# Output stage of a hybrid attention layer: SyncE and GpSimd in program order, weight splits spread over the tail of the attention

## The chip, the cores and the metric

The kernel runs on one core of a Trainium2 chip. The metric is the device time of one execution in microseconds. The core has five engines with queues of their own: TensorE (PE in the profile; its weight loads are PEld), VectorE (DVE), ScalarE (ACT), GpSimd (POOL) and SyncE (SP), which issues nearly all transfers here. Each engine runs its queue in order; semaphores let one engine wait for another or for a transfer.

## What is computed

One layer over two sequences, a prompt of 1024 rows and a sample of 2048, each row 1024 wide. The first half of the mixed features comes from a windowed attention, the second from a differential attention with an RMS norm over each head. Cut to what matters here:

```
mod = silu(c) @ w_ada + b_ada            # shift, scale, gate of a sequence
u = x * (1 + scale) + shift
qa, ka, va, ga, qb, kb, vb, gb = split(u @ w_in)
oa = window_gqa(qa, ka, va, sink, rel_bias) * silu(ga)              # 512 columns
ob = rms_norm(diff_attention(qb, kb, vb, ...)) * (1 - lambda_init) * silu(gb)   # 512 columns
h = concatenate([oa, ob]) @ w_out                                    # 1024 x 1024
y = layer_norm(ALPHA * x + gate * h, ln_g, ln_b)
```

Of this, the last two lines and the two products in front of them (the norm's factor and silu(gb)) are the output stage.

## The kernel before, in words

The program runs the projections (L186 to L188), the windowed attention, the differential attention and the output stage, in this order, and passes intermediate results through DRAM: oa (gated result of the windowed attention), ot (the differential attention before its norm), frow (the norm's factor of each row, written by 4-byte stores of f at L894), gb (silu of the gate).

The differential attention is cut into 80 units, 64 of the sample and then 16 of the prompt, in software-pipelined slots. `slot(n, ...)` runs the logits of unit n, the softmax of it, and the transposes (L852), values (L870 to L872) and sums (L885, L887) of units up to 3 slots earlier. The slots 80 to 85 are a tail without logits. In them, `slot` is handed a generator, `other`, and calls `next(other)` four times in each; when the slots are over, the rest of the generator is run out. The generator is `outputs()`.

`outputs()` runs the output stage over 24 tiles of 128 rows: first 16 of the sample (s = 1), then 8 of the prompt (s = 0). Tile t needs:
- `load_rest(t)`: five transfers on SP, ot (L999), frow (L1000, one row broadcast to all 128 partitions), gb (L1001), oa (L1002), 256 KB each in SBUF, and x (L1004), 512 KB. They go into 4 rotating buffers `l0`; x goes into 6 views named vt or ptl.
- `join(t)`: POOL multiplies ot by frow (L1012) and by gb (L1013), ACT rounds each half (L1016, half 0 from oa, half 1 from the product) to the high part, and POOL subtracts it (L1017, twice) for the low part. `os_` has three pairs of views for the results (names Q, pth, ptl).
- `output(B, end)`: two halves of 512 columns, each 24 matmuls of 128x512 (L1042 to L1044, high by high, high by low, low by high, 8 row blocks of w_out) in 16 steps, then on DVE the gate (L1047), the residual (L1048) and the norm's statistics (L1051, L1055, L1057). POOL computes the power for 1/sigma (L1058); DVE (L1080), ACT (L1082) and POOL (L1083) apply the norm to both halves, and SP stores the tile (L1084). Tile 23 has an end of its own (L1060 to L1076). PSUM holds the accumulators of two tiles.

In `output` of tile t, `load_rest(t + 3)` is written behind the third step and `join(t + 1)` behind the fifth.

`stage(ks)` loads rows of w_out (L975), `split_weights(k)` splits row block k into a high and a low part (L989 on DVE, L990 on ACT, L991 on POOL and DVE), `load_gate(s)` loads the gate row (L1023) and `load_norm()` the two norm rows (L1028), each broadcast to all partitions.

What sets the order: the program is written for a tile framework that orders the instructions of each engine by a simulated timeline of its own. Inside `tc.manual_schedule(engines=...)` the named engines keep the order in which the program is written. Before, in the last block this names PE alone, so SP, POOL, DVE and ACT follow the framework's order. A transfer waits on SP for the transfer eight places earlier to have landed, because eight semaphores are used in turn.

Of the kernel before, what the change touches and what calls it, by code (L numbers as in the profile page):

```python
# [15 lines left out]
PSUM = bass.MemoryType.PSUM  # L16
DRAM = bass.MemoryType.DRAM

PE = mybir.EngineType.PE
P = 128  # L20
D = 1024
KC = D // P
# [44 lines left out]
def hybrid_layer(ctx, tc, x_prompt, x_sample, c_prompt, c_sample, w_in, w_out, w_ada, b_ada, ln_g, ln_b,  # L67
# [314 lines left out]
    def project_until(cc, n):  # L382
        while done.get(cc, 0) < n:
            if next(steps, steps) is steps:
                break
# [30 lines left out]
    def load_ada(p):  # L416

        hs = []
        for kq in range(4):
            wt = wa_p.tile([P, 2, 2, 256], F32, tag="wa", name="wa")  # L420
            src = w_ada[kq * 256:(kq + 1) * 256, 0:2 * D].rearrange("(k p) (t n) -> p k t n", p=P, t=2)
            for t in range(2):
                ld = nc.sync.dma_start(out=wt[:, :, t, :], in_=src[:, :, t, p * 256:(p + 1) * 256])
            hs.append(wt)
        wada.append(hs + [ld.ins])
# [31 lines left out]
    load_ada(0)  # L457
    with tc.manual_schedule(engines={PE}):
        project_until(0, 6)
# [37 lines left out]

    with tc.manual_schedule(engines={PE}):
        project_until(0, 7)
# [28 lines left out]
    sst.close()  # L528
    with tc.manual_schedule(engines={PE}):
        project_until(0, 13)  # L530


    def windowed(upto):

        order = [(s, i) for s in (0, 1) for i in range(SEQS[s] // P)]
        NB = len(order)
        Bs, live, wait, n0 = {}, [], [], done.get(2, 0)
        total = (upto - n0) * 32
        Bs[0] = load_block(*order[0])
        count = [0, 0]  # L540

        def beside():
            count[0] += 1
            while count[1] * NB * 16 < count[0] * total and done.get(2, 0) < upto:
                next(steps, None)
                count[1] += 1

        for t in range(NB + 2):
            for n in range(2):
                if t < NB and order[t][0] == 1 and order[t][1] >= 7:  # L550
                    project_until(2, 5)
                f = first(Bs[t], n) if t < NB else iter(())
                for h4 in range(4):
                    next(f, None)
                    beside()
                    for g in list(live):
                        if next(g, live) is live:
                            live.remove(g)
                    beside()
                if t < NB:  # L560
                    wait.append(second(Bs[t], n))
                if len(wait) > 1 or t >= NB and wait:
                    live.append(wait.pop(0))
                if n == 0 and t + 1 < NB:
                    Bs[t + 1] = load_block(*order[t + 1])
        for g in live:
            for _ in g:
                pass
        project_until(2, upto)
# [95 lines left out]
    UPTO = 10  # L665
    with tc.manual_schedule(engines={PE}):
        project_until(1, 13)
# [13 lines left out]

    with tc.manual_schedule(engines={PE}):
        windowed(UPTO)
# [213 lines left out]
    def slot(n, extra, other=None):  # L897
        for j in range(4):
            if extra:
                fill(extra)  # L900
            if n < N:
                logits(n, j)
                prefetch(n, j)
            for g, piece in values_at.get(n, ()):
                if piece % 4 == j:
                    values(g, piece)
            if 0 <= n - LAG < N:
                transpose(n - LAG, j)
            if j == 1 and n in sums_at:
                square_sum(sums_at[n])  # L910
            if other is not None:
                next(other, None)
# [4 lines left out]
    ps_lg.open(lst, space=PSUM)  # L917
    with tc.manual_schedule(engines={PE}):
        for n in range(EARLY):
# [35 lines left out]
    def part():  # L955
        return weight(next(turn))
# [15 lines left out]
    def stage(ks):  # L972
        for k in ks:
            raws[k] = early_p.tile([P, D], F32, tag="wo", name="raw") if k < 4 else row_halves()
            nc.sync.dma_start(out=raws[k], in_=w_out[k * P:(k + 1) * P, :])  # L975
# [7 lines left out]
    def split_weights(k):  # L983
        woH[k], woL[k] = wmem[2 * k](), wmem[2 * k + 1]()
        raw = raws.pop(k)
        for n in range(2):
            ns = slice(n * 512, (n + 1) * 512)
            if k >= 4:
                nc.vector.tensor_scalar(out=raw[:, ns], in0=raw[:, ns], scalar1=wsub, scalar2=None, op0=ALU.mult)  # L989
            nc.scalar.copy(woH[k][:, ns], raw[:, ns])  # L990
            (nc.vector if n else nc.gpsimd).tensor_tensor(  # L991
                out=woL[k][:, ns], in0=raw[:, ns], in1=woH[k][:, ns].bitcast(F32), op=ALU.subtract)

    def load_rest(t):

        s, i = order[t]
        cs = slice(i * P, (i + 1) * P)
        d = dat.next().rearrange("p (n i q) -> p n i q", n=4, i=4)
        nc.sync.dma_start(out=d[:, 1], in_=OT[s][:, :, cs].rearrange("k r t -> r k t"))  # L999
        nc.sync.dma_start(out=d[:, 2], in_=frow[s][:, cs].partition_broadcast(P))  # L1000
        nc.sync.dma_start(out=d[:, 3], in_=GB[s][:, :, cs].rearrange("k r t -> r k t"))  # L1001
        nc.sync.dma_start(out=d[:, 0], in_=OA[s][:, :, cs].rearrange("i r t -> r i t"))  # L1002
        xt = xts.next().bitcast(F32)
        nc.sync.dma_start(out=xt, in_=xs[s][cs, :])  # L1004
        Bs[t] = dict(s=s, i=i, d=d, xt=xt)

    def join(t):

        B = Bs[t]
        d = B["d"]  # L1010
        B["oH"], B["oL"] = [v.rearrange("p (k q) -> p k q", k=KC) for v in os_.next()]
        nc.gpsimd.tensor_tensor(out=d[:, 1], in0=d[:, 1], in1=d[:, 2], op=ALU.mult)  # L1012
        nc.gpsimd.tensor_tensor(out=d[:, 1], in0=d[:, 1], in1=d[:, 3], op=ALU.mult)  # L1013
        for half in range(2):
            hs = slice(half * 4, half * 4 + 4)
            nc.scalar.copy(B["oH"][:, hs, :], d[:, half])  # L1016
            nc.gpsimd.tensor_tensor(out=B["oL"][:, hs, :], in0=d[:, half], in1=B["oH"][:, hs, :].bitcast(F32),  # L1017
                                    op=ALU.subtract)


    def load_gate(s):
        keep[s] = part().bitcast(F32)
        nc.sync.dma_start(out=keep[s], in_=grow[s, :].partition_broadcast(P))  # L1023

    def load_norm():
        for name, v in (("g", ln_g), ("b", ln_b)):
            keep[name] = part().bitcast(F32)
            nc.sync.dma_start(out=keep[name], in_=v.partition_broadcast(P))  # L1028
# [60 lines left out]

    def outputs():  # L1090

        load_rest(0)
        stage((4, 5, 6, 7))
        yield
        for k in range(3):
            split_weights(k)
            yield
        load_gate(1)
        load_norm()
        for k in range(3, 7):  # L1100
            split_weights(k)
            yield
        split_weights(7)
        load_rest(1)
        load_rest(2)
        join(0)
        for t in range(NB):
            if t == 8:
                load_gate(0)
            for j, _ in enumerate(output(Bs[t], t == NB - 1)):  # L1110
                if j == 2 and t + 3 < NB:
                    load_rest(t + 3)
                if j == 4 and t + 1 < NB:
                    join(t + 1)
                yield
            del Bs[t]
            yield
# [5 lines left out]
    lst.close()  # L1123
    ps_po = pool(st, "ps_po", 4, PSUM)
    other = outputs()
    with tc.manual_schedule(engines={PE}):
        for n in range(N, max(sums_at) + 1):
            slot(n, 0, other)
        for _ in other:
            pass  # L1130
# [27 lines left out]
```

## Time and profile before

| | us |
|---|---|
| median of 3 runs | 2199.94 |
| lowest, highest | 2194.16, 2206.9 |
| the profiled run | 2195.32 |
| span of the profiled run | 2193.5 |
| PE busy in it | 2081.7 (95%) |
| DVE, ACT, POOL busy | 1300.9, 1034.6, 1153.6 |

The output stage runs from about 1836 us (its first matmul) to the end, with the attention's tail under its first part. Rows of the profile read: start or time, duration in us, engine and line, out<-in by the names of the program. A mark in brackets at a row's end is the idle time of its engine ahead of it, and what ended it. Waits are told as sum in us, times, and longest.

### The profile page before, as it was taken

The page shows a single profiled execution, that of the slowest core. Times are in us where ns is not written, and L with a number is a line of the kernel's source. Part 1 is how long each engine was busy: PE and PEld are TensorE (multiplying, and loading weights), DVE is VectorE, ACT ScalarE, POOL GpSimd, SP SyncE. Part 2 cuts the span into 40 slices and gives each one's busy share as a digit, 9 for nine tenths or more (in the row PEclk, how much of TensorE's full clock was granted, in tenths as well). Part 3 has the DMA queues.
Part 4 walks back from the last instruction along what each step waited for, and adds up shares of the span by engine and source line. Part 5 has one row for each costly group of instructions (what it writes and reads, how often), then busy time and mean ns, then how long its engine had stood idle before and what let it go on. Part 6 is the DMA issues. An engine that isn't in the chain of part 4 may idle for free.

```text
span 2193.5 us, 32703 instructions
## 1 busy us (share of the span) xinstructions
PE 2081.7 (95%) x11597; PEld 1781.9 (81%) x11597; DVE 1300.9 (59%) x2538; ACT 1034.6 (47%) x2022; POOL 1153.6 (53%) x836
## 2 busy tenths in 40 slices
PE   7999999999999999999999999999999987588998
PEld 4777898888988788888978999999999876466777
DVE  6343124212245666767539999999999974244445
ACT  6211113111035677777428777777778973111221
POOL 3223123222233334433338898888989885455573
PEclk9999999999999999999999999999999998799999
DMA  9676536445449667786524231322214646755531
GB/s 279 178 273 181 161 130 178 120 130 135 149 142 241 181 181 196 199 224 160 158 78 132 75 81 37 98 66 81 75 47 132 113 99 173 145 152 162 168 127 58
DMA packets 340204, 312.46 MB, mean 142 GB/s; under 512 B 32087, under 2 KB 296951, under 8 KB 339657
## 3 DMA queue, kind: packets, MB, share of 16 engines
q1 hardware_dynamic: 340040, 310.37, 51.7%
q8 instruction: 92, 1.51, 0.4%
q14 instruction: 72, 0.58, 0.2%
HBM read 212.70 MB, written 97.60 MB: 141 GB/s over the span
## 4 chain that ended last, share of the span: by engine, by line
PE 74%; DMA 11%; POOL 5%; issue 4%; DVE 3%; SPq 2%; ACT 1%; DVEq 0%; POOLq 0%; ACTq 0%
PE lg L814 13%; PE pj L186 11%; PE pj L187 11%; PE pj L188 11%; PE tp L852 6%; PE ac L872 3%; PE ac L871 3%; PE ac L870 3%; PE lgA L607 3%; PE tp L643 2%; DMA l<-ot 2%; PE ac L635 2%; DMA Q<-qb 1%; PE po L1042 1%; PE ac L634 1%
## 5 line engine op out<-in xcount | busy, mean ns | idle before, releaser
L186 PE MATMUL pj<-uH,wH 128*128 128x512 f32 x1040 | 417.0, 401 | 3.8 <-DVE gg L257 3.8
L188 PE MATMUL pj<-uH,wL 128*128 128x512 f32 x1040 | 407.1, 391 | 0.0
L187 PE MATMUL pj<-uL,wH 128*128 128x512 f32 x1040 | 406.7, 391 | 0.0
L217 POOL TENSOR_TENSOR wL<-wr,wH 128x1024 fp32r<-128x1024 f32 x74 | 181.9, 2459 | 410.0 <-DVE wH L215 367.9
L814 PE MATMUL lg<-kt,Q 128*128 128x512 f32 x1280 | 377.9, 417 | 8.0 <-DMA Q<-qb 5.3
L838 POOL TENSOR_TENSOR l<-l,l 128x1024 f32<-128x1024 f32 x160 | 383.1, 2420 | 0.2
L827 ACT ACTIVATE l<-l,nm 128x2048 f32<-128x2048 f32 (+1 forms) x192 | 331.0, 1724 | 20.0 <-DVE nm L819 19.8
L814 PEld LDWEIGHTS lg<-kt,Q 128*128 128x128 f32 x1280 | 218.1, 190 | 40.4 <-issue 3.9
L819 DVE CUSTOM_DVE_ANT_0 l<-lg,W 128x1024 f32<-128x1024 f32 x192 | 233.4, 1216 | 17.8 <-PE lg L814 17.6
L854 ACT CAST pth<-tp 128x512 fp32r<-128x512 f32 x320 | 186.2, 582 | 115.8 <-PE tp L852 111.9
L836 POOL TENSOR_SCALAR l<-l,s 128x1024 f32<-128x1024 f32 x160 | 179.1, 1134 | 113.2 <-DVE s L832 56.0
L188 PEld LDWEIGHTS pj<-uH,wL 128*128 128x128 f32 x1040 | 195.1, 188 | 42.2
L186 PEld LDWEIGHTS pj<-uH,wH 128*128 128x128 f32 x1040 | 195.5, 188 | 35.8 <-DVE gg L257 4.6
L187 PEld LDWEIGHTS pj<-uL,wH 128*128 128x128 f32 x1040 | 195.8, 188 | 29.6
L855 DVE TENSOR_TENSOR ptl<-tp,pth 128x512 fp32r<-128x512 f32 x320 | 208.9, 684 | 11.3 <-ACT pth L854 10.3
L852 PE MATMUL tp<-ident,l 128*128 128x128 f32 x1280 | 194.9, 276 | 8.7 <-DVE ptl L855 8.6
L870 PE MATMUL ac<-pth,vt 128*128 128x256 f32 x640 | 182.1, 285 | 5.9 <-ACT ac L887 5.9
L622 POOL TENSOR_SCALAR l<-l,rcA 128x384 f32<-128x384 f32 (+1 forms) x144 | 81.1, 581 | 196.5 <-PE ac L634 93.9
L872 PE MATMUL ac<-pth,vt 128*128 128x256 f32 x640 | 183.0, 286 | 0.0
L871 PE MATMUL ac<-ptl,vt 128*128 128x256 f32 x640 | 182.6, 285 | 0.0
L819 DVE CUSTOM_DVE_ANT_0 l<-lg,W,nm 128x1024 f32<-128x1024 f32 x128 | 164.1, 1282 | 23.3 <-PE lg L814 15.9
L852 PEld LDWEIGHTS tp<-ident,l 128*128 128x128 f32 x1280 | 149.9, 142 | 11.8 <-DVE ptl L855 3.8
(209 smaller groups left out, 4048.1 us busy)
## 6 DMA issues: line engine op xcount, KB each, us to landing
wr<-in_w_in SPq DMA_DIRECT2D x39, 1024.0 KB, 5.5
KAt<-ka SPq DMA_DIRECT2D x40, 384.0 KB, 10.0
QAt<-qa SPq DMA_DIRECT2D x24, 512.0 KB, 4.3
kt<-kb SPq DMA_DIRECT2D x24, 512.0 KB, 9.0
Q<-qb SPq DMA_DIRECT2D x48, 256.0 KB, 3.0
Q<-qb SPq DMA_DIRECT2D x96, 128.0 KB, 4.0
vt<-vb SPq DMA_DIRECT2D x48, 256.0 KB, 5.7
out<-vt SPq DMA_DIRECT2D x20, 512.0 KB, 2.6
```

The lines of the kernel that those rows point to most:

```text
L186: nc.tensor.matmul(acc, lhsT=a(k), rhs=b(k), start=(k == 0), stop=False)
L187: nc.tensor.matmul(acc, lhsT=a(k), rhs=bl(k), start=False, stop=False)
L188: nc.tensor.matmul(acc, lhsT=al(k), rhs=b(k), start=False, stop=(k == KC - 1))
L814: nc.tensor.matmul(L[:, c * CH:(c + 1) * CH], lhsT=G["Q"][:, v, m, b * P:(b + 1) * P], rhs=Kt[kt0 + c][:, m, :], start=(v == 0), stop=(v = ...
L819: nc.vector.tensor_tensor_reduce(out=half, in0=L, in1=W[:, off:off + 1024], scale=1.0, scalar=nm[:, m, 0:1] if s and hf else 3e38, op0=ALU ...
L827: nc.scalar.activation(e, e, AF.Exp, bias=nm[:, m, hf:hf + 1], scale=-1.0, accum_out=sums)
L838: nc.gpsimd.tensor_tensor(out=row[:, cs], in0=row[:, cs], in1=rows[n][1][:, cs], op=ALU.add)
L852: nc.tensor.transpose(pt[:, c * P:(c + 1) * P], rows[n][0][:, (j * 4 + c) * P:(j * 4 + c + 1) * P], ident)
L855: nc.vector.tensor_tensor(out=L[:, :, qs], in0=p3, in1=H[:, :, qs].bitcast(F32), op=ALU.subtract)
L870: nc.tensor.matmul(a, lhsT=Vt[kq][:, 0, c, :], rhs=H[:, c, :], start=(kb == 0), stop=False)
L871: nc.tensor.matmul(a, lhsT=Vt[kq][:, 0, c, :], rhs=L[:, c, :], start=False, stop=False)
L872: nc.tensor.matmul(a, lhsT=Vt[kq][:, 1, c, :], rhs=H[:, c, :], start=False, stop=(kb == T - 1))
```

## The change

In `outputs()`, the loads of the rows of w_out 4 to 7 are put before the first `load_rest`. The splits 0 to 3 take a step each, then come the gate row, two empty steps, the norm rows, and another step. The splits 4 to 7 follow at one step each, with join(0) and load_rest(1) behind split 5, and load_rest(2) behind the last. Tile 0 starts after 12 steps instead of 8, in slot 83 instead of 82. And in the last block SP and POOL keep the program's order, like PE; DVE and ACT do not.

```diff
@@ -16,7 +16,7 @@
 PSUM = bass.MemoryType.PSUM
 DRAM = bass.MemoryType.DRAM
 
-PE = mybir.EngineType.PE
+PE, SP, POOL = mybir.EngineType.PE, mybir.EngineType.SP, mybir.EngineType.Pool
 P = 128
 D = 1024
 KC = D // P
@@ -1089,21 +1089,24 @@
 
     def outputs():
 
+        stage((4, 5, 6, 7))
         load_rest(0)
-        stage((4, 5, 6, 7))
         yield
-        for k in range(3):
+        for k in range(4):
             split_weights(k)
             yield
         load_gate(1)
+        yield
+        yield
         load_norm()
-        for k in range(3, 7):
+        yield
+        for k in range(4, KC):
             split_weights(k)
+            if k == 5:
+                join(0)
+                load_rest(1)
             yield
-        split_weights(7)
-        load_rest(1)
         load_rest(2)
-        join(0)
         for t in range(NB):
             if t == 8:
                 load_gate(0)
@@ -1123,7 +1126,7 @@
     lst.close()
     ps_po = pool(st, "ps_po", 4, PSUM)
     other = outputs()
-    with tc.manual_schedule(engines={PE}):
+    with tc.manual_schedule(engines={PE, SP, POOL}):
         for n in range(N, max(sums_at) + 1):
             slot(n, 0, other)
         for _ in other:
```

On SP, at the first store of an output tile: the rows around `out_1`, the sample's output. The names at the left are what is written; l0 with a number is the buffer of one tile's loads, ot1, frow1, gb1 and oa1 are the sample's DRAM tensors, vt and ptl hold x, and ot0 and frow0 belong to the prompt's attention. Before:

```order
L1002 DMA l0_19129<-oa1_99 128x4x128
L999 DMA l0_19064<-ot1_98 128x4x128
L894 DMA frow0_102<-f_19277 128x2x1
L1001 DMA l0_18843<-gb1_97 128x4x128
L999 DMA l0_19129<-ot1_98 128x4x128
L1000 DMA l0_19057<-frow1_103 128x4x128
L1001 DMA l0_19057<-gb1_97 128x4x128
L1084 DMA out_1<-vt_18848 128x1024
L1002 DMA l0_18843<-oa1_99 128x4x128
L1000 DMA l0_19064<-frow1_103 128x4x128
L1004 DMA vt_18848<-in_x_sample 128x1024
L999 DMA l0_18843<-ot1_98 128x4x128
```

After:

```order
L1000 DMA l0_19175<-frow1_103 128x4x128
L1001 DMA l0_19175<-gb1_97 128x4x128
L1002 DMA l0_19175<-oa1_99 128x4x128
L1004 DMA vt_19180<-in_x_sample 128x1024
L876 DMA ot0_81<-osb_19188 128x256
L894 DMA frow0_102<-f_19223 128x2x1
L876 DMA ot0_81<-osb_19247 128x256
L894 DMA frow0_102<-f_19265 128x2x1
L1084 DMA out_1<-vt_18854 128x1024
L999 DMA l0_18849<-ot1_98 128x4x128
L1000 DMA l0_18849<-frow1_103 128x4x128
L1001 DMA l0_18849<-gb1_97 128x4x128
```

Before, the first store stands among loads of four different buffers, in mixed order; now the five loads of a tile stand together, behind the store of a tile before it.

On ACT, from the norm of tile 3 on (`L1016 CAST` is a half of a join, `L1082 ACTIVATE` a half of the norm; l0 with a number is again a buffer of loads). Before:

```order
L1082 ACTIVATE vt_19134<-po_19472,ve_19541 128x512
L1082 ACTIVATE vt_19134<-po_19511,ve_19541 128x512
L1016 CAST ptl_19165<-l0_19129 128x512 x2
L1082 ACTIVATE vt_19322<-po_19552,ve_19621 128x512
L1082 ACTIVATE vt_19322<-po_19591,ve_19621 128x512
L1016 CAST ptl_19330<-l0_18843 128x512 x2
L1082 ACTIVATE ptl_19405<-po_19632,ve_19701 128x512
L1082 ACTIVATE ptl_19405<-po_19671,ve_19701 128x512
```

After:

```order
L1082 ACTIVATE vt_19180<-po_19472,ve_19541 128x512
L1082 ACTIVATE vt_19180<-po_19511,ve_19541 128x512
L1016 CAST ptl_19330<-l0_19075 128x512
L1016 CAST ptl_19204<-l0_19175 128x512
L1082 ACTIVATE vt_19322<-po_19552,ve_19621 128x512
L1082 ACTIVATE vt_19322<-po_19591,ve_19621 128x512
L1016 CAST Q_19067<-l0_19134 128x512
L1016 CAST ptl_19330<-l0_18849 128x512
```

vt_19134 and vt_19180 are tile 3, vt_19322 is tile 4 in both. Before, the two L1016 of one join stand between the norms of two tiles; now there are halves of two different joins: between tiles 3 and 4 half 1 of tile 5 (l0_19075) and half 0 of tile 7 (l0_19175).

On POOL, around the powers of the tiles 3 and 4 (ve_19541 and ve_19621; L1058 is the power, L1083 the norm's last step, L1012, L1013 and L1017 the join). Before:

```order
L1058 TENSOR_TENSOR ve_19461<-ve_19461,mhalf_109 128x1
L1012 TENSOR_TENSOR l0_19057<-l0_19057 128x512
L1083 TENSOR_TENSOR vt_19069<-vt_19069,pth_18949 128x512 x2
L1013 TENSOR_TENSOR l0_19057<-l0_19057 128x512
L1017 TENSOR_TENSOR Q_19072<-l0_19064,Q_19071 128x512 x2
L1058 TENSOR_TENSOR ve_19541<-ve_19541,mhalf_109 128x1
L1083 TENSOR_TENSOR vt_19134<-vt_19134,pth_18949 128x512 x2
L1012 TENSOR_TENSOR l0_19064<-l0_19064 128x512
L1017 TENSOR_TENSOR pth_19166<-l0_19129,ptl_19165 128x512
L1013 TENSOR_TENSOR l0_19064<-l0_19064 128x512
```

After:

```order
L1013 TENSOR_TENSOR l0_18849<-l0_18849 128x512
L1017 TENSOR_TENSOR pth_19205<-l0_18849,ptl_19204 128x512 x2
L1058 TENSOR_TENSOR ve_19541<-ve_19541,mhalf_109 128x1
L1083 TENSOR_TENSOR vt_19180<-vt_19180,pth_19009 128x512 x2
L1012 TENSOR_TENSOR l0_19075<-l0_19075 128x512
L1013 TENSOR_TENSOR l0_19075<-l0_19075 128x512
L1017 TENSOR_TENSOR pth_19331<-l0_19075,ptl_19330 128x512 x2
L1058 TENSOR_TENSOR ve_19621<-ve_19621,mhalf_109 128x1
L1083 TENSOR_TENSOR vt_19322<-vt_19322,pth_19009 128x512 x2
L1012 TENSOR_TENSOR l0_19134<-l0_19134 128x512
L1013 TENSOR_TENSOR l0_19134<-l0_19134 128x512
```

The join of one tile, from L1012 to the second L1017, now stands whole behind the norm of another; before, its parts stand ahead of, between and behind the norm's.

## Rows read from the trace of the kernel before

**Rows 1.** Windows: us, busy time of each engine (instructions), PEclk, DMA share, GB/s

```profile
1836.00:1867.00 31.00, 26.68 (x153) 23.41 (x152) 7.81 (x16) 9.68 (x30) 14.37 (x14) 0.94 0.72 186
1867.00:1906.00 39.00, 19.04 (x82) 14.79 (x80) 15.55 (x28) 3.00 (x6) 14.72 (x14) 0.79 0.76 133
1906.00:2000.00 94.00, 72.59 (x272) 56.91 (x273) 30.78 (x53) 13.75 (x24) 52.59 (x46) 0.87 0.56 155
2000.00:2130.00 130.00, 120.65 (x499) 95.00 (x498) 59.91 (x102) 24.09 (x42) 82.92 (x74) 0.97 0.49 153
```

**Rows 2.** Waits of PE, ACT and POOL in the output stage: total us, times, longest

```profile
PE po L1042 <- ACT vt L1082: 47.1, 11, 23.8
ACT vt L1082 <- POOL ve L1058: 191.5, 16, 32.9
POOL l L1012 <- DMA l<-ot: 110.6, 20, 17.5
```

**Rows 3.** Timeline of SP, and the chain of waits: start us, us, what

```profile
1953.36 0.36 SPq L1000 DMA_DIRECT2D l<-frow  x1
...
1957.06 9.13 DMA l<-ot
```

**Rows 4.** Timeline: the longest wait of POOL, and stores issued on SP

```profile
1893.14 1.26 POOL L1012 TENSOR_TENSOR l<-l 128x512 f32<-128x512 f32 x1 [17.55 <-DMA l<-ot]
1905.73 1.24 SPq L1084 DMA_DIRECT2D out<-vt  x1
2075.79 0.35 SPq L1084 DMA_DIRECT2D out<-vt  x1
2159.08 0.33 SPq L1084 DMA_DIRECT2D out<-vt  x1
2181.28 0.33 SPq L1084 DMA_DIRECT2D out<-vt  x1
2189.77 1.08 SPq L1076 DMA_DIRECT2D out<-ptl  x2
```

**Rows 5.** Transfers issued (1923, 2034, 1982 us on; page): KB, us to landing

```profile
l<-frow SPq DMA_DIRECT2D x1, 256.0 KB, 8.2
l<-frow SPq DMA_DIRECT2D x1, 256.0 KB, 4.7
l<-gb SPq DMA_DIRECT2D x8, 256.0 KB, 3.4
out<-vt SPq DMA_DIRECT2D x20, 512.0 KB, 2.6
```

**Rows 6.** Windows of a few us, columns as above

```profile
1954.00:1960.00 6.00, 2.82 (x9) 1.99 (x9) 3.78 (x7) 2.29 (x4) 5.20 (x6) 0.85 0.24 38
1961.00:1965.00 4.00, 4.00 (x18) 3.21 (x17) 0.00 (x0) 0.00 (x0) 0.00 (x0) 0.93 1.03 339
1996.00:1999.00 3.00, 3.00 (x15) 2.42 (x14) 0.47 (x1) 0.00 (x0) 3.00 (x3) 1.00 0.31 78
```

**Rows 7.** Timeline: single instructions of a tile on POOL, SP and ACT

```profile
2008.33 2.54 POOL L1083 TENSOR_TENSOR vt<-vt,pth 128x512 f32<-128x512 f32 x2
2014.88 0.39 SPq L999 DMA_DIRECT2D l<-ot  x1
2015.15 1.27 ACT L1082 ACTIVATE vt<-po,ve 128x512 f32<-128x512 f32 x2 [10.57 <-POOL ve L1058]
2016.30 1.14 ACT L1016 CAST Q<-l 128x512 fp32r<-128x512 f32 x2
```

**Rows 8.** The attention's tail: a wait of SP, timeline, chain, first output matmul

```profile
SPq L999 <- PE tp L852: 10.1, 1, 10.1
1818.64 1.26 POOL L1012 TENSOR_TENSOR l<-l 128x512 f32<-128x512 f32 x1 [7.80 <-DMA l<-frow]
1836.00 0.48 PE L1042 MATMUL po<-kt,Q 128*128 128x512 f32 x1
1859.21 8.29 DMA frow<-f
1867.99 18.76 DMA frow<-f
```

## The prediction

> **What bounds the kernel now.** I read the windows of the output stage first [rows 1], then the waits of the engines there [rows 2], then the chain [rows 3], and last the rows of single instructions. The windows show that PE is the bound nowhere before 2000 us: from 1867 to 1906 it works 19.04 of 39 us, from 1906 to 2000 72.59 of 94, and from 2000 to 2130 120.65 of 130, where the granted clock is 0.97, so the 2.4 GHz level nearly throughout. The waits say what it lacks. PE waits 47.1 us for free PSUM tiles, which the ACT normalisation at L1082 gives back; ACT waits 191.5 us there for the POOL power at L1058; POOL waits 110.6 us in L1012 for a load [rows 2]. POOL runs in order, and L1012, the first product of a later tile's join, stands ahead of the small power of a tile that is ready, so a late load holds up both. The worst case is the hole of 17.55 us before the L1012 at 1893.14. The first store, out(0), leaves at 1905.73, out(12) at 2075.79, out(20) at 2159.08, and the program's last at 2189.77 [rows 4]. That is 170.1 us for the twelve cycles up to out(12), 14.2 each, 83.3 us for the next eight, 10.4 each, and the rest.
>
> Late loads are the kernel's real price here. The broadcast frow (512-byte pieces, one row for all partitions) is slow: 256 KB of the sample's land 8.2 us after issue, of the prompt's 4.7, whereas 256 KB of gb take 3.4 and a 512 KB store 2.6 [rows 5]. While only a sample's frow is under way (1954 to 1960) the queues move 38 GB/s, with a prompt's (1996 to 1999) 78, and right behind it (1961 to 1965) 339 [rows 6]. Loads of one queue land in the order of issue: the ot issued at 1957.06 landed 9.13 later, at 1966.19 [rows 3]. Behind the frow that left at 1953.36 there were 1.28 MB (oa, x, gb, ot), 3.8 us at 339 GB/s, so this frow landed near 1962.4, 9.0 us after issue. I take 9.0 for the sample's, with 8.2 as the lower bound and 9.7 as the upper (9.13 and half a handover), and 4.7 for the prompt's. What hides this now is that the loads run two or three tiles ahead of their use, in whatever order the scheduler gave SP.
>
> **The change part by part.** *Manual order on SP.* The added load order is strictly out(t-1), then the five loads of tile t+3: ot, frow, gb, oa, x. No load is ahead of a store any more, although nothing but the scheduler's order made it so; the work saved is nil (the same DMAs, 0.35 to 0.4 us of issue each). *Manual order on POOL.* Per tile: L1058, L1083 twice, then the next join's L1012, L1013 and L1017 twice. The long L1012 waits of POOL [rows 2] therefore no longer stand between a finished tile and its power. Alone that would give back up to 110.6 us of POOL wait, of which PE feels only its 47.1 us. *ACT stays with the scheduler, and there a wait appears.* In its new row L1016 of tile t+3, half 0, which reads oa(t+3), stands ahead of the L1082 of tile t. In the old one L1082 stood ahead of it. Now oa(t+3) is issued behind out(t-1), so a loop closes: out(t-1) is issued, oa(t+3) lands, L1016, L1082 and L1083 of tile t run, out(t) is issued. Queued behind the waiting L1016 on ACT are both L1082 of tile t; behind these wait POOL's L1083 and SP's store, and PE for PSUM.
>
> The period of that loop for a sample's tile: two issues up to frow's own 0.9, at some 0.4 each [rows 7], frow 9.0, gb and oa 0.5 MB at 339 GB/s 1.6, one half of L1016 0.6 and one of L1082 0.65, both halves of L1083 2.54 [rows 7], and five handovers of 0.1, which is 15.8 us. (A frow of 8.2 gives 15.0, one of 9.7 gives 16.5.) For a prompt's it is 11.5. PE needs 11.1 per tile ((2181.28 - 2159.08)/2, out(20) to out(22), PE without pause [rows 4]), so the loop is later than PE in both, by 4.7 and 0.4 us.
>
> Stores issued: tiles out(0) to out(12) trigger the loads of tiles 4 to 15, all sample; those up to out(20) the prompt's. Twelve cycles at 15.8 are 190 against 170.1 now: **+19.5**. Eight at 11.5 are 92 against 83.3: **+8.7**. Behind out(20) nothing is loaded any more, and PE, the join and the two last tiles run as they do now: **0**.
>
> *Order in the tail.* Loads of tiles 0 to 3, the gate, the norm rows and the splits are spread; output(0) gets its first PE steps four steps (one slot) later than now. Two stalls go: SP no longer waits 10.1 us at L999 for the transposes of PE at L852, and POOL no longer 7.8 us before L1012 at 1818.64 with L836 behind it. Two come: the loads of the last rows of w_out stand behind stores of f, 4-byte packets, one of which took 8.29 us [rows 8]. I set these against each other at 0, with 6 us either way. Then ACT's L1082 of tile 0 waits, by the same inversion, for oa of tile 3. By then the queue has to move, from about 1841 (when the sums of the slot let SP go on; first output matmul at 1836.00 [rows 8]), gate and norm rows 1.5 MB, tiles 1 and 2 3.0, ot to oa of tile 3 1.0, attention stores 0.4: 5.9 MB. The windows from 1836 to 1906 give (31 x 186 + 39 x 133)/70 = 156 GB/s [rows 1], so 38 us: oa(3) at 1879, out(0) near 1884 instead of 1905.73: **-21.7**. What covers this is that nothing else needs the queue; without the cover (oa(3) only by 1900) the gain is gone.
>
> The sum: -21.7 + 19.5 + 8.7 + 0 = +6.5 us against the profiled run's own 2195.32, of which 2193.5 are span. The three runs' median is 4.6 us above that, so on its scale 2199.94 + 6.5 = **2206**. PE idle of before, 47 us, is not won, because the wait only changes its owner.
>
> The Trainium skill bears on that step ("DMA: Bandwidth & Descriptors", section "Queues, rings and completion order"): descriptors of one ring are consumed in order on each engine. That speaks against the change, since oa must then wait behind out and frow, and rows 3 agree.
>
> **The rivals.** *A, faster: the loop is later than nothing.* If a frow that is alone behind a store lands as other loads of its size do, in 3.4 us, the period is 10.2, below PE's 11.1, and PE sets the pace. Then out(0) at 1884, 20 x 11.1, and 34.4 from out(20) to the end: a span of 2140, a run of 2142, 2147 on the median. For it: frow's neighbours share the 16 engines, and GB/s is high right behind it. Against it: 38 GB/s in a stretch with nothing else in the queue [rows 6]. The Trainium skill has a rule for it, the fit of 2.0 us and bytes/436e3 in "DMA: Bandwidth & Descriptors", "Anatomy of one DMA — SWDGE (gpsimd) path": by it 256 KB take an estimated 2.6 us, and the case would be A. Rows 5 disagree, for gb by 0.8 us and for frow by more. Chance 0.18.
> *M, in between:* frow at the 6 to 7 us of a mean of both kinds, or the loop slackened by a store that leaves early: 13 to 14 us a cycle, and -21.7 - 14 + 8.7 or -21.7 - 2 + 8.7: 2173 to 2185. Chance 0.14.
> *B, slower: out(0) isn't earlier.* SP in the order of the program puts the loads of tiles 1 to 3 behind stores of f, whose data come from DVE and POOL at the end of each slot. Each such store holds SP until its data are there, and the chain has one that took 18.76 us, at 1867.99 [rows 8]. It decides if oa(3) lands after 1900: then the -21.7 falls away, the loop still costs +28, and the time is 2228; with frow at 9.7 2236. Chance 0.18.
> That the change does nothing is excluded, since the rows of SP, POOL and ACT are in another order.
>
> **How the numbers follow.** Forecast 0.50 (2192 to 2220: out(0) 10 us either way, a frow between the bounds), A 0.18, M 0.14, B 0.18. Half a per cent, about what a measurement tells from no change, is 11 us, so same is 2189 to 2211. Faster gets A, nearly all of M, and none of the forecast: 0.31. Of the forecast 0.32 lies within the 11 us and 0.18 above, B lies above: same 0.32, slower 0.37. As both signs have much chance, the range goes from A's 2147 to B's 2232, and 2192 to 2220 is the likeliest case's own.
>
> **What would show it.** Right: ACT's largest wait is L1016 on a load of oa, some 8 us, in twelve tiles; stores out(t) 16 us apart for tiles 1 to 12 and 11.5 after; out(0) near 1884; no POOL wait in L1012 for a load; a granted clock below 0.9 up to out(12), since PE pauses 4.7 us in each tile. Wrong if stores are 11.1 apart from the start (A) or if out(0) leaves after 1895 (B), or if frow in the new queue lands in less than 6 us.

## The result, and the profile after

The changed kernel takes 2262.78 us (median of 4 runs, 2257.25 to 2264.41) against 2197.88 for the one before; the ratio is 1.0285, with a 95% interval of 1.0248 to 1.0322. The forecast was 2206 and the range ended at 2232: the direction was right, the size far too small. The profiled runs differ by nearly as much: spans of 2255.5 and 2193.5 us, 62.0 apart.

First the timeline of SP, the stores of tiles 0, 12 and 20, which answer to the stores of [rows 4].

```profile
1904.25 0.34 SPq L1084 DMA_DIRECT2D out<-vt  x1
...
2110.22 0.35 SPq L1084 DMA_DIRECT2D out<-vt  x1
...
2220.92 0.35 SPq L1084 DMA_DIRECT2D out<-vt  x1
```

They place the loss: the first store comes 1.5 us earlier than before, the twelve cycles up to out(12) take 206.0 us instead of 170.1 (17.2 each), the next eight 110.7 instead of 83.3 (13.8 each), and the rest 34.6 instead of 34.4. -1.5 + 35.9 + 27.4 + 0.2 = 62.0. All of the loss is in the cycles.

The windows of the three stretches, with the columns of [rows 1] (busy us of PE, PEld, DVE, ACT, POOL; PEclk, DMA share, GB/s):

```profile
1836.00:1904.00 68.00, 41.92 (x203) 35.25 (x201) 17.66 (x33) 12.78 (x38) 23.47 (x22) 0.80 0.68 101
1904.00:2110.00 206.00, 154.38 (x576) 119.91 (x576) 70.05 (x120) 28.87 (x48) 95.88 (x85) 0.89 0.48 125
2110.00:2221.00 111.00, 92.95 (x380) 73.08 (x381) 46.63 (x80) 19.25 (x32) 64.69 (x58) 0.97 0.53 152
```

No engine is full, PE pauses about 4.3 us in each of the twelve cycles, and the queues move less than before (125 GB/s against 155 in the third of rows 1). Something is waited for in turn. The waits from out(0) on, ACT's up to out(20), say what; they answer to [rows 2]:

```profile
PE po L1044 <- POOL pth L1017: 49.9, 14, 5.6
PE po L1044 <- POOL Q L1017: 22.1, 7, 5.6
...
POOL vt L1083 <- ACT vt L1082: 131.8, 19, 9.9
POOL ptl L1083 <- ACT ptl L1082: 24.3, 3, 9.5
...
ACT ptl L1016 <- DMA l<-oa: 121.8, 14, 11.0
...
ACT Q L1016 <- DMA l<-oa: 53.9, 6, 10.3
```

POOL's waits in L1012, 110.6 us before, are gone from here on (one of 18.1 us, for a frow, is left in the tail), and PE waits only 0.7 us for PSUM. In their place ACT stands in L1016 for oa 20 times, 175.7 us in all, POOL's L1083 waits for ACT's L1082 behind it, and PE for the join that POOL reaches only then. The chain of waits shows one turn of the loop, from the issue of an oa (2.5 us behind out(3)) to the issue of the next:

```profile
1957.55 11.57 DMA l<-oa
...
1969.23 0.06 ACT ptl L1016
...
1969.75 0.69 ACT vt L1082
...
1971.75 1.27 POOL vt L1083
1973.02 0.02 issue
1973.03 0.35 SPq L1084
...
1974.21 0.60 SPq L1000
1974.81 0.05 issue
1974.86 0.69 SPq L1001
1975.55 0.04 issue
1975.59 11.10 DMA l<-oa
```

The load of oa, one half of L1016, the norm, the store, three issues of loads (ot, frow, gb), and the next load of oa: this is the loop of the prediction, link by link. What is longer than forecast is its first link. The transfers between 1921 and 2112 us (sample) and between 2113 and 2195 us (prompt), with median us from issue to landing, answer to [rows 5]:

```profile
l<-ot SPq DMA_DIRECT2D x12, 256.0 KB, 3.6
l<-frow SPq DMA_DIRECT2D x12, 256.0 KB, 10.6
...
l<-oa SPq DMA_DIRECT2D x11, 256.0 KB, 10.7
...
l<-oa SPq DMA_DIRECT2D x6, 256.0 KB, 7.3
...
l<-frow SPq DMA_DIRECT2D x6, 256.0 KB, 7.1
```

A sample's ot is there 3.6 us after its issue, its frow, issued 0.5 us later, after 10.6: 7.5 us from the one landing to the next.

### The profile page after: what moved, and what is told of

It is laid out like the page before. It is cut to its first block, busy times and chain, and to the rows that moved or that the text cites. A ratio compares the mean times of both kernels' runs of the same rounds, so it can differ in the third digit from the quotient of the medians.

```text
span 2255.5 us, 32659 instructions
## 1 busy us (share of the span) xinstructions
PE 2099.9 (93%) x11597; PEld 1793.1 (80%) x11597; DVE 1296.5 (57%) x2538; ACT 1037.2 (46%) x2022; POOL 1154.6 (51%) x836
## 4 chain that ended last, share of the span: by engine, by line
PE 70%; DMA 16%; SPq 4%; DVE 3%; POOL 3%; issue 2%; ACT 1%; ACTq 0%; DVEq 0%; POOLq 0%
PE lg L814 12%; PE pj L186 11%; PE pj L187 11%; PE pj L188 11%; DMA l<-oa 8%; PE tp L852 5%; PE ac L872 3%; PE ac L871 3%; PE ac L870 3%; PE lgA L607 3%; PE tp L643 2%; DMA Q<-qb 2%; PE ac L635 2%; POOL vt L1083 1%; PE ac L634 1%
## 5 line engine op out<-in xcount | busy, mean ns | idle before, releaser
L814 PE MATMUL lg<-kt,Q 128*128 128x512 f32 x1280 | 377.2, 416 | 8.3 <-DMA Q<-qb 6.1
L814 PEld LDWEIGHTS lg<-kt,Q 128*128 128x128 f32 x1280 | 217.3, 190 | 40.8 <-issue 6.6
L855 DVE TENSOR_TENSOR ptl<-tp,pth 128x512 fp32r<-128x512 f32 x320 | 208.7, 684 | 12.1 <-ACT pth L854 10.8
L852 PE MATMUL tp<-ident,l 128*128 128x128 f32 x1280 | 195.9, 276 | 17.1 <-DVE ptl L855 17.0
```

Source lines behind the costliest of these rows:

```text
L814: nc.tensor.matmul(L[:, c * CH:(c + 1) * CH], lhsT=G["Q"][:, v, m, b * P:(b + 1) * P], rhs=Kt[kt0 + c][:, m, :], start=(v == 0), stop=(v = ...
L852: nc.tensor.transpose(pt[:, c * P:(c + 1) * P], rows[n][0][:, (j * 4 + c) * P:(j * 4 + c + 1) * P], ident)
L855: nc.vector.tensor_tensor(out=L[:, :, qs], in0=p3, in1=H[:, :, qs].bitcast(F32), op=ALU.subtract)
```

## The experiments

Each edit is against the changed kernel unless another is named, and times are medians beside the kernel before on the same chip (2198.56 to 2202.54).

**Which engine's order makes the loss?** Three kernels change only what follows the program.

```diff
-    with tc.manual_schedule(engines={PE, SP, POOL}):
+    with tc.manual_schedule(engines={PE, SP}):        # e_sp
+    with tc.manual_schedule(engines={PE, POOL}):      # e_pool
+    with tc.manual_schedule(engines={PE}):            # e_spread
```

> The changed kernel, but in the last block only PE and SP keep the program's order; POOL goes back to the scheduler. Loop theory (store of tile t-1, then load of tile t+3 on SP, whose oa half ACT rounds ahead of the norm of tile t): the loop needs SP's order and ACT's order, not POOL's, so the stores stay 17 us apart for the sample and 13.8 for the prompt, and the time within 12 us of the changed kernel's 2263. Rival (POOL's order makes the loss): stores 14 us apart as before, near 2200.

Measured: 2272.01 (ratio 1.0319, 1.0298 to 1.034), stores 18.0 us apart up to out(12) and 14.7 behind it. The loss is there without POOL's order. Why each cycle is 0.8 to 0.9 us longer than in the changed kernel was not followed up.

> The changed kernel, but only PE and POOL keep the program's order; SP goes back to the scheduler, which puts the loads of six tiles ahead of the first store and load of tile t+6 behind the store of t. Loop theory: no loop although ACT still rounds half 0 of tile t+3 ahead of the norm of tile t; no ACT wait for oa above 2 us in the steady part, stores at the pace of the transfers, near 13 us for the sample, and at PE's 11.1 for the prompt: 2180 to 2200. Rival (POOL's order makes the loss): stays near 2263.

Measured: 2144.31 (0.9753, 0.9728 to 0.9778), 118 us below the changed kernel and, level with e_poolpad below, the fastest of all. Its window from out(0) to out(20) has PE without a gap:

```profile
1887.00:2108.00 221.00, 221.00 (x956) 179.08 (x955) 116.59 (x199) 50.51 (x80) 161.78 (x139) 1.00 0.68 183
```

From out(1) to out(20) the stores are 10.7 us apart on the mean. This was below the 2180 that I expected: the transfers, which I had put at 13 us a tile, don't set the pace there, they carry 183 GB/s. ACT's order has the same inversion in this kernel; what differs is that the load of tile t+6, not t+3, stands behind the store of t.

> The changed kernel with only PE in the order of the program: the spread of the splits and loads alone. Loop theory: the loads are hoisted again, the stores 14 us apart as in the kernel before, and the time within 20 us of its 2198. Rival (the spread of the splits makes the loss by a late start): first store after 1925 us and a time above 2230.

Measured: 2197.26 (0.9973, 0.9953 to 0.9992): the spread alone does next to nothing, and POOL waits in L1012 for ot again.

```profile
POOL l L1012 <- DMA l<-ot: 106.2, 19, 21.6
```

**Is the loop closed by ACT's order?** Here ACT too follows the program, in which tile t's norm comes behind the join of tile t+1, not behind half of that of t+3.

```diff
-    with tc.manual_schedule(engines={PE, SP, POOL}):
+    with tc.manual_schedule(engines={PE, SP, POOL, ACT}):
```

> The changed kernel, with ACT too in the order of the program, so that ACT rounds tile t+1, not t+3, ahead of the norm of tile t; the orders of SP and POOL stay as changed. Loop theory: the oa in question was issued two stores earlier, the loop is gone, stores near 13 us apart for the sample and 11.1 for the prompt, 2180 to 2200, PE waits for the join under 1 us a tile. Rival (the strict order of SP alone costs it, each load late behind a store whoever waits): ACT or POOL waits for the load instead, stores still 16 us or more apart, over 2240.

Measured: 2163.36 (0.9825, 0.981 to 0.9839), with stores 9 to 12.6 us apart from tile 2 on. In the cycles SP's strict order costs nothing by itself: out(0) to out(20) takes 218.7 us, against 221.3 in e_pool. As with e_pool the pace came out faster than I had expected, and PE sets it (busy for 192.93 of the 193 us from out(2) to out(20)). The time is still 19 us above e_pool's. In the two profiles this lies ahead of out(0), which leaves at 1908.48 here and at 1886.80 there; why was not followed up.

**Can the loop be opened elsewhere?** One kernel loads a tile earlier, one loads oa first.

```diff
-                if j == 2 and t + 3 < NB:
-                    load_rest(t + 3)
+                if j == 2 and t + 4 < NB:
+                    load_rest(t + 4)
...
         load_rest(2)
+        load_rest(3)
```

> The changed kernel with the loads of tile t+4, not t+3, written behind the third step of tile t (and those of tile 3 put with tile 2's). SP, POOL in program order and ACT's inversion stay. Loop theory: the loop now spans two stores, so its period of 17 us is shared by two tiles and PE's 11.1 us decide: stores 11 us apart from tile 2 on, 2155 to 2175 in all. Rival (the order of SP as such costs it): stores stay over 15 us apart, over 2230.

Measured: 2170.2 (0.9866, 0.9847 to 0.9885), stores 11.1 apart from tile 4 on.

```diff
+        nc.sync.dma_start(out=d[:, 0], in_=OA[s][:, :, cs].rearrange("i r t -> r i t"))
         nc.sync.dma_start(out=d[:, 1], in_=OT[s][:, :, cs].rearrange("k r t -> r k t"))
         nc.sync.dma_start(out=d[:, 2], in_=frow[s][:, cs].partition_broadcast(P))
         nc.sync.dma_start(out=d[:, 3], in_=GB[s][:, :, cs].rearrange("k r t -> r k t"))
-        nc.sync.dma_start(out=d[:, 0], in_=OA[s][:, :, cs].rearrange("i r t -> r i t"))
```

> The changed kernel with oa as the first of a tile's five loads instead of the fourth. Every order between tiles stays. Loop theory with the frow as its long term: the loop loses ot, frow and gb, some 8 us of its 17, falls below PE's 11.1, and the time to 2155 to 2180. Rival (the wait is for the store ahead, or a fixed time of any transfer): stores still over 14 us apart, over 2215.

Measured: 2172.42 (0.9871, 0.9855 to 0.9888), stores 11.1 apart from tile 4 on. Moving one line of five takes back all of the loss and more. Both were as expected.

**What in the load is long?** The first kernel replaces the broadcast of frow by a plain load of as many bytes, the second keeps it and sets frow's rows 512 bytes further apart in DRAM.

```diff
-        nc.sync.dma_start(out=d[:, 2], in_=frow[s][:, cs].partition_broadcast(P))
+        nc.sync.dma_start(out=d[:, 2], in_=GB[s][:, :, cs].rearrange("k r t -> r k t"))
```

> The changed kernel with the frow load replaced by a second load of gb's rows, of the same 256 KB without the broadcast (so the norm's factor is left out and the result differs). Theory: the broadcast is the slow part, about 7.5 us between the landings of ot and frow; a load of the plain kind takes 0.9 there, so the period falls from 17.2 to about 10.6 for the sample and below PE's 11.1 for the prompt: stores 11 us apart, 2155 to 2175. Rival (any 256 KB load behind a store takes this long): stores 16 us apart, over 2240.

Measured: 2161.41 (0.9823, 0.9802 to 0.9844), stores 11 to 12 us apart in most cycles. The transfer itself is not slow by its size or its place behind a store.

```diff
-    frow = [dt_([HB, S], f"frow{s}") for s, S in enumerate(SEQS)]
+    frow = [dt_([HB, S + P], f"frow{s}") for s, S in enumerate(SEQS)]
```

> The changed kernel with frow's rows 512 bytes further apart in DRAM (pitch 8704 and 4608 bytes instead of 8192 and 4096). If the pitch makes the sample's broadcast slower than the prompt's, the sample's stores come 14 us apart or less instead of 17.2, and the time falls to 2225 or below. Rival (slow because 128 partitions read the same lines, whatever the pitch): 17 us, within 10 us of 2263.

Measured: 2175.24 (0.9887, 0.9859 to 0.9915), stores 12.3 us apart for the sample and for the prompt. I had given 14. The transfers of this kernel from 1904 to 2088 us:

```profile
l<-ot SPq DMA_DIRECT2D x15, 256.0 KB, 3.6
l<-frow SPq DMA_DIRECT2D x15, 256.0 KB, 5.2
```

The same broadcast of the same bytes lands 5.2 us after issue instead of 10.6, some 2 us behind ot instead of 7.5. So it is the layout of frow in DRAM, with 8192 bytes between the four rows, that makes the sample's broadcast slow. For the prompt's, with 4096 bytes, this trace has no time to landing, but its cycles fell too, from 13.8 to 12.3 us. Only one wider pitch was tried, and why the pitch matters is not shown. The loop is still the bound, since 12.3 is above PE's pace, but at 28% less for the sample and 11% less for the prompt. The Trainium skill has a fact of this kind ("DMA: Bandwidth & Descriptors", section "Latency and other measured facts", row on the pitch of rows at large powers of two): there, copies at pitches of 2 MiB and more are slowed, and 4 KiB added to a pitch of 4 MiB restores their rate, while 192 bytes do not. This case's runs agree in kind (10.6 us to landing against 5.2), at a pitch of 8 KiB and with 512 bytes added, neither of which that row covers.

The kernel before, and then e_pool, with the wider pitch (the same edit):

> The kernel before with the wider pitch alone. If the slow broadcast set its pace of 14.2 us up to out(12) and its late first store, POOL's waits for loads in L1012 fall from 110.6 us to under 50 and the time to 2150 to 2175. Rival (the scheduler's order of POOL sets it): 2185 to 2200.

Measured: 2169.72 (0.9868, 0.985 to 0.9886), inside the range. Up to out(12) the stores came 11.9 us apart instead of 14.2. Out(0) left at 1908.20, but in this run the attention ended late (its last matmuls of logits, L814, start at 1822.44, in the profile of before at 1803.12); from there it is 85.8 us instead of 102.6. POOL's waits for ot fell from 110.6 us only to 62.7, not below 50, so its order keeps a share:

```profile
POOL l L1012 <- DMA l<-ot: 62.7, 18, 5.1
POOL l L1012 <- DMA l<-frow: 23.7, 4, 13.0
```

> PE and POOL alone in the order of the program (2144), with the wider pitch. The stores there are already 10.9 us apart, which is PE's pace, so only the start can gain: out(0) 0 to 15 us before 1886.8, 2130 to 2145.

Measured: 2144.58 (0.9762, 0.9737 to 0.9786), the same as e_pool, at the upper end of what was expected. Out(0) leaves at 1882.78 instead of 1886.80 and the profiled span is 2139.7 instead of 2142.6 us, a gain too small for these runs to tell.

**Does the order in the tail matter?** The old order is put back, once with SP, POOL and PE in the order of the program (e_oldorder), once with POOL and PE (e_oldpool).

```diff
+        load_rest(0)
         stage((4, 5, 6, 7))
-        load_rest(0)
         yield
-        for k in range(4):
+        for k in range(3):
...
-            if k == 5:
-                join(0)
-                load_rest(1)
             yield
+        split_weights(7)
+        load_rest(1)
         load_rest(2)
+        join(0)
```

> The old order of splits and loads in the tail with SP, POOL and PE in the order of the program. Loop theory: the same loop, stores 17.1 and 13.8 us apart, and the time within 25 us of the changed kernel's 2263, by what the tail gives or takes. Rival (the spread is what costs): near 2200.

Measured: 2253.29 (1.0241, 1.022 to 1.0261): stores 17.3 us apart up to out(12) and 13.9 behind it. The loop is the same with the old tail, and the time 9 us lower.

> The old order of splits and loads with PE and POOL in the order of the program, SP with the scheduler. If POOL's order is the gain (the power no longer behind a join that waits for its load), stores 11 us apart and 2140 to 2165; if the spread of the splits is needed for it, above 2180.

Measured: 2149.12 (0.9764, 0.9736 to 0.9791), as with the new tail. POOL has no wait for a load in L1012 in this trace. The gain comes with POOL's order; the spread is not needed for it. With POOL's order set, the scheduler orders SP and ACT otherwise too: SP issues 6 loads of oa ahead of the first store and ACT runs 6 casts (L1016) ahead of the first norm (L1082), where the kernel before has 8 and 8. What this is worth by itself was not separated.

**Why was the first store late?** The tail's stores of f go to ACT's queue (with `tail` set ahead of the last block).

```diff
-        nc.sync.dma_start(out=frow[s][h, i * P:i * P + QG].rearrange("(b p) -> p b", p=P), in_=f[:, 4:6])
+        (nc.scalar if tail else nc.sync).dma_start(out=frow[s][h, i * P:i * P + QG]..., in_=f[:, 4:6])
```

> The changed kernel with the stores of f in the tail's slots issued from ACT's queue instead of SP's. Theory for the start that was not won (the loads of tiles 1 to 3 land in order behind the stores of f on SP's queue, each of which takes 8 to 19 us to land): oa of tile 3 lands some 15 us earlier, so out(0) leaves near 1888 instead of 1904.3, and the loop is as it was: 2240 to 2255. Rival (the queue is slow with the sheer bytes of the tail, 156 GB/s): out(0) within 5 us of 1904, 2257 to 2268.

Measured: 2250.23 (1.0228, 1.0199 to 1.0256), out(0) at 1894.91. I had given 1888. In this run the tail began later than in the changed kernel's, so the start is better counted from a mark. From the same store of f (1820.53 and 1815.13) it is 74.4 us instead of 89.1, 14.7 less, and the wider pitch alone (e_frowpad) gives 71.4. But SP reaches that store only after a wait for POOL, which took 8.4 us here, 6.1 in the changed kernel and 10.8 in e_frowpad. The attention's last matmuls of logits lie ahead of that wait: they start at 1809.41, 1806.33 and 1806.46, and out(0) leaves 85.5, 97.9 and 85.0 us later. So the gain is 12.4 us here and 12.9 with the pitch. SP's waits for the data of f, 17.4 us in three waits up to out(0) of the changed kernel, leave its queue with the stores, so this run does not tell them from the slow landings.

With the wider pitch as well:

> The changed kernel with the wider pitch of frow and the tail's stores of f on ACT's queue. If both held the loads of tiles 1 to 3, out(0) leaves another 5 to 10 us earlier than with the pitch alone (counted from the store of f in slot 80, 71 us there): 60 to 66 us; stores 12.2 apart as with the pitch alone; 2165 to 2172. If the f stores are hidden once the broadcast is quick, 71 us and 2172 to 2178.

Measured: 2178.4 (0.9908, 0.9875 to 0.994), out(0) at 1900.62, 75.4 us behind that store and 86.3 behind the last logits (1814.31). Together they win no more than each alone, as in the second case of the expectation. ACT's timeline at the norm of tile 0 shows why. In the changed kernel:

```profile
1900.42 0.62 ACT L1016 CAST Q<-l 128x512 fp32r<-128x512 f32 x1 [14.03 <-DMA l<-oa]
1900.94 1.26 ACT L1082 ACTIVATE vt<-po,ve 128x512 f32<-128x512 f32 x2
```

And in e_fq, then in e_padfq, where the norm's line is L1084:

```profile
1891.56 1.29 ACT L1084 ACTIVATE vt<-po,ve 128x512 f32<-128x512 f32 x2 [5.26 <-DVE po L1082]
...
1897.28 1.29 ACT L1084 ACTIVATE vt<-po,ve 128x512 f32<-128x512 f32 x2 [5.26 <-DVE po L1082]
```

With the stores of f out of the way, the norm of tile 0 no longer waits for oa of tile 3 but for VectorE's step of the same norm, so an earlier oa of tile 3 has nothing more to give.

And the same edit in e_pool:

> PE and POOL alone in the order of the program (2144), and the tail's stores of f on ACT's queue. If the stores of f hold the loads in the tail, out(0) leaves 5 to 15 us before the 1886.8 of that kernel and the time is 2130 to 2140; if ACT's queue or its own order gets in the way, or the loads weren't late, 2142 to 2155.

Measured: 2163.55 (0.9833, 0.98 to 0.9865), out(0) at 1911.95, a miss: 19 us slower than e_pool. From the last logits to out(0) it is 95.0 us, against 78.5 in e_pool. The store of f on ACT's queue is no gain where SP issues the loads that early. Whether ACT's issue of it or the scheduler's new order did it was not separated.

## Why the prediction was wrong, point by point

**The loop: right, but for one reading.** It was named with its links, its waiting engine and who is held behind it; e_act, e_ahead4 and e_oafirst each open or shorten one link, and the loss is gone each time, while e_sp and e_oldorder keep the links and the loss. ACT's waits for oa came to 8.8 us on the mean, where some 8 were given. The wrong reading is that in ACT's old row the norm of tile t stood ahead of the cast of tile t+3. In the trace of before ACT runs 8 casts, those of four tiles, ahead of the first norm, so the inversion was there already; the changed kernel runs 6 and e_pool 6. What the change added is the place of the load: SP issues 8 loads of oa ahead of the first store before, 4 in the changed kernel, 5 in e_ahead4 and 6 in e_pool. The loop needs both, the cast ahead of the norm and its load right behind the store of the tile before.

**Its period: the step that failed.** The prediction counted 9.0 us for a sample's frow and 4.7 for a prompt's from the frow's own issue. It took them from transfers before [rows 3, 5] that SP had issued 5 us or more behind the transfer ahead of them. In the loop every frow is issued 0.9 us behind a 512 KB store and 0.5 behind an ot, which land 3.1 and 3.6 us after their issues, and the sample's frow lands 7.5 us behind that ot. Measured from issue it is 10.6 and 7.1, in both cases 2.4 us more than in [rows 5] (8.2 and 4.7). That the broadcast starts only when the store and the ot are through is inferred from this and was not seen itself. The sum of links is then 0.9 + 10.6 + 1.7 (to oa's landing, 2.5 + 10.7 behind the store) + 3.9 = 17.1 for the sample and 0.9 + 7.1 + 1.8 + 3.9 = 13.7 for the prompt; 17.2 and 13.8 were measured. The rest of the loop was put at 4.3 us and took 3.9. The error per cycle looks small, 1.4 and 2.3 us, but it counts 12 and 8 times: (17.16 - 15.8) x 12 + (13.84 - 11.5) x 8 = 16 + 19 = 35 us.

**The start: the gain was not there.** Out(0) was put at 1884 and left at 1904.25: 20 us, of which 3.2 are that the attention ended later in this run (its last logits at 1806.33, before at 1803.12). The order of events was right, since the last thing that out(0) waited for is oa of tile 3, through the same inversion. The rate was wrong: I took 156 GB/s from the same time before [rows 1], and the queues moved 101 (first window above); 5.9 MB at 101 GB/s are 58 us from 1841, which is 1899, and that oa landed at 1900.34. The rows of the chain in the tail:

```profile
1840.29 13.55 DMA pth<-grow
...
1853.88 10.50 SPq L1002
...
1878.65 0.70 SPq L999
...
1881.67 18.67 DMA l<-oa
```

The rate says how late, not why. One thing in the tail that the prediction did not have (it set the stalls there against each other at 0) is the same inversion ahead of the attention's own work, a cast for a later tile in front of L875 on ACT:

```profile
1873.84 0.62 ACT L1016 CAST ptl<-l 128x512 fp32r<-128x512 f32 x1 [22.16 <-DMA l<-oa]
1874.36 0.36 ACT L875 COPY osb<-ac 128x256 f32<-128x256 f32 x1
```

PE waits 22.3 us for L875 in two waits, 18.3 of it in the longer; what this adds to the 20 us was not separated.

Rival B named stores of f ahead of the loads as the mechanism and 1900 as its point, and this is what came, with two causes: e_fq and e_frowpad show that taking away either the stores of f or the pitch of frow wins 12 to 13 us, and e_padfq that both together win no more, because tile 0's own end is next. How the 20 us divide between them remains open.

**Together:** 35 + 20 = 55 us over the forecast's 2201.8 on the profiled run's scale, and 2257.25 came. The start alone would have stayed in the range (2226), the period alone would have passed its end by 9 us (2241). B was priced with the loop of the forecast, so that its 2228 lacked the 35 us.

**POOL's order: right in its mechanism, missed in its worth.** The text said that POOL's L1012 in front of the power is the wait of before, that the new order takes it away, and that the loop eats what it gives. e_pool and e_oldpool show the worth, 58 and 49 us (with the orders that the scheduler then gives SP and ACT), where I had taken PE's 47.1 us of PSUM waits as the most. In e_pool's profile out(0) leaves 18.9 us earlier than before, and the cycles to out(20) take 221.3 us instead of 253.4.

**The rivals.** A was wrong since the broadcast is slow here; with a plain load the time (2161) is near A's 2147. The fit from the Trainium skill that the prediction quotes for A stands there for transfers that GpSimd issues, and the loads here are issued by SP; a plain load of 256 KB took 3.4 to 3.6 us. M did not occur.

## What to carry to other kernels

When an order by hand is set on some of the engines, look at the rows of those that stay with a scheduler. Here ACT rounded a load three tiles ahead in front of the norm, which did no harm as long as that load was issued early. Once SP issued it right behind the store of the tile before, a loop of 17 us closed, and any one of four edits (e_pool, e_act, e_ahead4, e_oafirst) undid it. Price a transfer in such a loop from the issue of what stands ahead of it in the queue, not from its own issue in a quiet stretch. And of a loop, check the period twice, since it is multiplied by the tiles.

## What was not expected of the hardware

The broadcast of four 512-byte pieces to 128 partitions landed 7.5 us behind the transfer ahead of it with rows 8192 bytes apart, and about 2 with rows 8704 bytes apart; the wider pitch alone made the kernel before 30 us faster (2199.64 to 2169.72) and the changed one 88 (2262.78 to 2175.24). The granted clock was 0.89 over the twelve sample cycles of the changed kernel, in each of which PE pauses (0.97 over the prompt's eight), and 1.00 (the 2.4 GHz level throughout) in e_pool, where it does not pause.
